# Loading the last columns of a batched matmul trace through another DMA queue

What was changed: the last 640 columns of the last B tile are loaded in float32 by SyncE instead of in bf16 by GpSimd, not before the last whole rows have landed, and VectorE multiplies them as they are.

## Chip, cores, metric

The program uses one core of one Trainium2 chip; its runs were spread over several chips, so each time is compared with the kernel before in the same rounds on the same chip. The metric is the device time of a run in microseconds (us). "Span" is the time from the first to the last instruction of the one profiled execution; it lies about 1.8 us below the run's time. PE is TensorE, PSUM the memory that it writes to, and a load has "landed" when the profile shows it complete. Times to a hundredth of a us that no printed line shows were read from the packed traces.

## The reference

```python
B, N = 8, 2176
prod = np.matmul(a, b)                                    # a, b: (8, 2176, 2176) float32
traces = np.diagonal(prod, axis1=1, axis2=2).sum(axis=-1) # (8,)
```

Only the trace is wanted, so each result is the sum of A-transposed times B, element by element: 2 x 151.5 MB are read once, and a handful of operations fall on each element.

## The kernel before

A is loaded with a cast to bf16 by GpSimd, transposed on PE into PSUM and copied ("evacuated") to `at`. B is loaded the same way. In the last batch B's products are shared: VectorE multiplies and sums (`multiply_reduce`, one column of `late` or `acc` per product), and PE accumulates 128x128 products in `trace_ps`, whose diagonal VectorE takes by a product with the identity. The last B row tile arrives in three pieces:

```python
LAST_PIECES = [(0, 2), (2, 3), (3, 5)]            # in units of 512 columns: 1024, 512, 640
...
for g0, g1 in LAST_PIECES:
    lo, hi = g0 * WIDE, min(g1 * WIDE, N)
    nc.gpsimd.dma_start(out=row[:, lo:hi], in_=b[bi, start:start + P, lo:hi])
multiply_on_pe(at, row, v0, 0, 1)
late.append((wide_at(at, v0, 1, 2), wide(row, 1, 2)))            # 512 columns on VectorE
for g in range(2, n_wide):                                        # 256 of each later 512
    half = ROWS // 2
    multiply_on_pe(at, row, v0, g, g + 1, rows=half)
    late.append((wide_at(at, v0, g, g + 1)[:, half:, :], wide(row, g, g + 1)[:, half:, :]))
multiply_on_pe(at, row, v0, n_wide, len(a_groups))
...                                                               # (cut)
for n, (x, y) in enumerate(late):
    multiply_reduce(x, y, late_acc[:, n:n + 1])
multiply_reduce(tiles[f32], trace_ps, late_acc[:, len(late):len(late) + 1])
...                                                               # sum over partitions on PE
nc.vector.tensor_copy(out=tiles["result"][:1, :BATCH], in_=total) # the "result copy"
nc.sync.dma_start(out=..., in_=tiles["result"][:1, :BATCH])       # the output
```

## Time and profile before

| | before |
|---|---|
| time, median of 4 runs | 711.43 us (711.36 to 711.58) |
| span of the profiled run | 709.8 us |
| HBM read over the span | 427 GB/s |
| VectorE / PE busy | 58% / 33% |
| last GpSimd piece seen / result copy / output issued | 705.60 / 706.91 / 707.10 us |

Read it like this: DMA bounds the whole stream, and the only part in which this change can alter the time is the last 7 us. The lines stand in the prediction.

### The profile page before, as it was taken

How to read it: one execution, taken by the hardware profiler on the slowest of the kernel's cores; microseconds unless marked ns; L12 is line 12 of the kernel's file. 1: busy time of each engine (PE TensorE's matmuls, PEld its weight loads, DVE VectorE, ACT ScalarE, POOL GpSimd, SP SyncE). 2: the span in 40 equal slices, each digit the busy share in tenths (PEclk: the TensorE clock that was granted, in tenths of full speed). 3: DMA queues.
4: the chain of work that ended last, by engine and by line, in shares of the span. 5: the costliest groups of instructions: out<-in, count | busy, mean ns of one | idle time of the engine just before them, and what ended most of it. 6: DMA issues, size and time to landing. Idle time of an engine off the chain costs nothing.

```text
span 709.8 us, 3800 instructions
## 1 busy us (share of the span) xinstructions
PE 233.3 (33%) x1406; PEld 221.8 (31%) x1406; DVE 408.9 (58%) x449; ACT 201.6 (28%) x210; POOL 45.2 (6%) x91
## 2 busy tenths in 40 slices
PE   2660025600345003540036400374003630036356
PEld 1660025600344003540036400374003630036355
DVE  0327972279812898219972199621996319963146
ACT  2651015600256002550035500354003630036300
POOL 2000000000000000000000000000000000000010
PEclk9866556755588555885556755666556875567755
DMA  9999999999999999999999999999999999999997
GB/s 220 220 220 219 206 219 219 220 218 206 221 219 218 218 210 218 220 218 214 213 219 219 218 213 214 220 218 216 213 217 219 218 216 212 218 218 216 219 210 139
DMA packets 12116, 152.32 MB, mean 215 GB/s; under 512 B 1346, under 2 KB 1602, under 8 KB 3778
## 3 DMA queue, kind: packets, MB, share of 16 engines
q0 software_dynamic: 11952, 150.97, 100.1%
q1 hardware_dynamic: 146, 1.11, 0.4%
q8 instruction: 11, 0.18, 0.1%
q14 instruction: 7, 0.06, 0.0%
HBM read 303.04 MB, written 0.00 MB: 427 GB/s over the span
## 4 chain that ended last, share of the span: by engine, by line
DMA 52%; issue 43%; POOL 3%; PE 2%; DVE 1%; another core or an unknown queue 0%; POOLq 0%; DVEq 0%
DMA t<-in_a_dram 42%; DMA t<-in_b_dram 6%; DMA b_t<-in_b_dram 3%; POOL t L57 2%; PE ps L136 1%; PE trace_ps L256 1%; DVE scratch L103 0%; DVE at L91 0%; POOL b_t L222 0%; POOLq L57 0%; PE ps L157 0%; POOL identity masks.py:199 0%; PE total L271 0%; POOL identity masks.py:197 0%
## 5 line engine op out<-in xcount | busy, mean ns | idle before, releaser
L103 DVE CUSTOM_DVE_ANT_1 scratch<-at,t 128x2048 bf16<-128x2048 bf16 (+1 forms) x156 | 310.5, 1990 | 85.5 <-DMA t<-in_b_dram 78.9
L136 PE MATMUL ps<-identity,t 128*128 128x128 f32 x1071 | 204.2, 372 | 460.3 <-DMA t<-in_a_dram 297.7
L136 PEld LDWEIGHTS ps<-identity,t 128*128 128x128 f32 x1071 | 193.7, 218 | 468.3 <-issue 302.8
L93 ACT COPY at<-ps 128x1024 bf16<-128x1024 bf16 x208 | 199.2, 1016 | 471.2 <-PE ps L136 471.1
L91 DVE COPY at<-ps 128x1024 bf16<-128x1024 bf16 (+2 forms) x104 | 92.8, 902 | 205.8 <-PE ps L136 198.9
L57 POOL DMA_DIRECT2D t<-in_a_dram x39 | 20.8, 535 | 329.5 <-DVE acc L103 230.2
L57 POOL DMA_DIRECT2D t<-in_b_dram x41 | 21.7, 530 | 304.2 <-PE ps L157 286.5
L256 PEld LDWEIGHTS <-at 128*128 128x128 bf16 x153 | 17.4, 124 | 12.0 <-issue 12.0
L256 PE MATMUL trace_ps<-t,at 128*128 128x128 bf16 x144 | 17.3, 294 | 10.2 <-DMA t<-in_b_dram 10.2
L157 PE MATMUL ps<-identity,t 128*128 128x128 bf16 x170 | 17.0, 224 | 2.2 <-DVE at L91 2.2
L157 PEld LDWEIGHTS <-t 128*128 128x128 bf16 x170 | 13.4, 102 | 3.8 <-issue 3.4
L103 DVE DVE_READ_ACCUMULATOR2_ANT acc<- 128x1 f32 x163 | 13.3, 82 | 0.0
L68 DVE CAST t<-words 128x1088 bf16<-128x1088 f32 x1 | 0.7, 726 | 4.9 <-DMA words<-in_a_dram 4.9
L103 DVE CUSTOM_DVE_ANT_0 scratch<-at,t 128x128 bf16<-128x128 bf16 x7 | 2.0, 291 | 0.2
L67 ACT CAST t<-words 128x1088 bf16<-128x1088 f32 x1 | 1.1, 1098 | 3.7 <-DMA words<-in_a_dram 3.7
L222 POOL DMA_DIRECT2D b_t<-in_b_dram x3 | 1.6, 539 | 3.6 <-PE trace_ps L256 3.6
L256 PE MATMUL trace_ps<-b_t,at 128*128 128x128 bf16 x9 | 1.5, 287 | 0.5 <-DMA b_t<-in_b_dram 0.4
L103 DVE CUSTOM_DVE_ANT_1 scratch<-at,b_t 128x256 bf16<-128x256 bf16 (+1 forms) x3 | 1.5, 510 | 0.2 <-DMA b_t<-in_b_dram 0.2
L248 DVE TENSOR_REDUCE sums<-acc 128x1 f32<-128x22 f32 (+1 forms) x8 | 1.4, 174 | 0.3
L67 ACT ACT_TABLE_LOAD x1 | 1.3, 1283 | 0.7 <-PEq L294 0.7
L271 PE MATMUL total<-late,ones 128*1 128x1 f32 x8 | 0.5, 163 | 0.3 <-DVE late L103 0.3
masks.py:199 POOL TENSOR_SCALAR_AFFINE_SELECT identity<-identity 128x128 f32<-128x128 f32 (+1 forms) x2 | 0.6, 308 | 0.0
(14 smaller groups left out, 2.4 us busy)
## 6 DMA issues: line engine op xcount, KB each, us to landing
t<-in_a_dram POOLq DMA_DIRECT2D x32, 2176.0 KB, 42.3
t<-in_b_dram POOLq DMA_DIRECT2D x31, 2176.0 KB, 47.2
t<-in_b_dram POOLq DMA_DIRECT2D x9, 544.0 KB, 39.5
t<-in_a_dram POOLq DMA_DIRECT2D x7, 544.0 KB, 35.0
words<-in_a_dram SPq DMA_DIRECT2D x1, 1088.0 KB, 5.0
t<-in_b_dram POOLq DMA_DIRECT2D x1, 1088.0 KB, 41.7
b_t<-in_b_dram POOLq DMA_DIRECT2D x1, 256.0 KB, 23.0
b_t<-in_b_dram POOLq DMA_DIRECT2D x1, 160.0 KB, 23.4
```

The lines of the kernel that those rows point to most:

```text
L57: issued = nc.gpsimd.dma_start(out=t[:, 0:m, :], in_=rows)
L67: nc.scalar.copy(out=t[:, 0, :half], in_=plain[:, :half])
L68: nc.vector.tensor_copy(out=t[:, 0, half:], in_=plain[:, half:])
L91: nc.vector.tensor_copy(out=dst, in_=src)
L93: nc.scalar.copy(out=dst, in_=src)
L103: nc.vector.tensor_tensor_reduce(out=out, in0=x, in1=y, scale=1.0, scalar=0.0, op0=MUL, op1=ADD, accum_out=acc,)
L136: nc.tensor.transpose(ps[:, n * m + r, :], words[:, r, c0:c0 + step * (P - 1) + 1:step], tiles[f32],)
L157: last_transpose = nc.tensor.transpose(ps16[:, n, r, :], a_t[:, r, c0:c0 + P], tiles[bf16],)
L222: nc.gpsimd.dma_start(out=row[:, lo:hi], in_=b[bi, start:start + P, lo:hi])
L248: nc.vector.reduce_sum(out=tiles["sums"][:, bi:bi + 1], in_=acc[:, :cols], axis=mybir.AxisListType.X)
L256: nc.tensor.matmul(trace_ps, x, y, start=(n == 0), stop=(n == len(pe_work) - 1),)
L271: nc.tensor.matmul(total[:, BATCH - 1:BATCH], tiles["ones"], part, start=(n == 0), stop=(n == len(parts) - 1),)
```

## The change

The intent: the last piece no longer needs PE and the accumulated matrix after it, and no longer goes through GpSimd's queue. Cut to its core:

```diff
-    LAST_PIECES = [(0, 2), (2, 3), (3, 5)]
+    LAST_ROUNDED = [(0, 1024), (1024, 1536)]
+    LAST_PLAIN = [(1536, 1920), (1920, N)]
+    plain_pool = ctx.enter_context(tc.tile_pool(name="plain", bufs=1))
...  # transpose_group: the last row of at is evacuated in column order (step of four elements)
+            if v0 == natural and m > 1:
+                in_order = at[:, v0, start:start + P * m].rearrange("q (p r) -> q r p", r=m)
+                evacuate(in_order, ps16[:, 0, :, :])
...  # last tile
+                for lo, hi in LAST_ROUNDED:
                     nc.gpsimd.dma_start(out=row[:, lo:hi], in_=b[bi, start:start + P, lo:hi])
+                    half = (lo + hi) // 2
+                    for c in range(lo, half, P):
+                        pe_work.append((at[:, v0, c:c + P], row[:, c:c + P]))
+                    late.append((at[:, v0, half:hi], row[:, half:hi]))
+                plain = plain_pool.tile([P, N - base], f32, tag="plain")
+                for lo, hi in LAST_PLAIN:
+                    begun = nc.sync.dma_start(out=plain[:, lo - base:hi - base], in_=b[bi, ..., lo:hi])
+                    tc.add_manual_dep(begun.ins, last_rows.ins.name, ...)   # after the last whole rows
+                    final.append((at[:, v0, lo:hi], plain[:, lo - base:hi - base]))
...  # after the identity product
+    for n, (x, y) in enumerate(final, len(late) + 1):
+        multiply_reduce(x, y, late_acc[:, n:n + 1])
```

More of the change, by code (lines that the diff above doesn't have):

```diff
@@ L80, in constants @@
         sums = const.tile([P, BATCH], f32, tag="sums")
-        late = const.tile([P, 4], f32, tag="late")
+        late = const.tile([P, 8], f32, tag="late")
         result = const.tile([P, BATCH], f32, tag="result")
@@ L111, with transpose_group @@
     split = n_wide * WIDE
-    def transpose_group(at, a_t, start, m, b_groups):
+    def transpose_group(at, a_t, start, m, b_groups, natural=None):
         words = a_t[:, :, :].bitcast(f32)
@@ L150, in transpose_group @@
                 evacuate(dst[:, v0:v0 + 2, :, :], halves[:, 0, :, :, :])
-        for at0 in range(0, len(singles), 8 // m):
-            some = singles[at0:at0 + 8 // m]
+        chunks = [singles[n:n + 8 // m] for n in range(0, len(singles), 8 // m)]
+        for some in chunks:
             ps = psum_pool.tile([P, 4, P], f32, tag="aT")
@@ L162, in transpose_group @@
             v0 = some[0][0]
-            evacuate(dst[:, v0:v0 + len(some), :, :], ps16[:, 0:len(some), :, :])
+            if v0 == natural and m > 1:
+                assert len(some) == 1
+                in_order = at[:, v0, start:start + P * m].rearrange("q (p r) -> q r p", r=m)
+                evacuate(in_order, ps16[:, 0, :, :])
+            else:
+                evacuate(dst[:, v0:v0 + len(some), :, :], ps16[:, 0:len(some), :, :])
         return last_transpose
@@ L184, in multiply_on_pe @@
                 ))
-    late = []
+    late, final = [], []
     ahead = None
@@ L204 @@
                 a_t, _ = load(a[bi], start, m)
-            last_transpose = transpose_group(at, a_t, start, m, b_groups)
+            last_transpose = transpose_group(
+                at, a_t, start, m, b_groups, natural=NT - 1 if last else None
+            )
         acc = acc_pool.tile([P, 2 * NT], f32, tag="acc")
@@ L219 @@
                 row = b_t[:, 0, :]
-                for g0, g1 in LAST_PIECES:
-                    lo, hi = g0 * WIDE, min(g1 * WIDE, N)
+                for lo, hi in LAST_ROUNDED:
                     nc.gpsimd.dma_start(out=row[:, lo:hi], in_=b[bi, start:start + P, lo:hi])
-                multiply_on_pe(at, row, v0, 0, 1)
-                late.append((wide_at(at, v0, 1, 2), wide(row, 1, 2)))
-                for g in range(2, n_wide):
-                    half = ROWS // 2
-                    multiply_on_pe(at, row, v0, g, g + 1, rows=half)
-                    late.append((
-                        wide_at(at, v0, g, g + 1)[:, half:, :], wide(row, g, g + 1)[:, half:, :]
-                    ))
-                multiply_on_pe(at, row, v0, n_wide, len(a_groups))
+                    half = (lo + hi) // 2
+                    for c in range(lo, half, P):
+                        pe_work.append((at[:, v0, c:c + P], row[:, c:c + P]))
+                    late.append((at[:, v0, half:hi], row[:, half:hi]))
+                base = LAST_PLAIN[0][0]
+                plain = plain_pool.tile([P, N - base], f32, tag="plain")
+                for lo, hi in LAST_PLAIN:
+                    begun = nc.sync.dma_start(
+                        out=plain[:, lo - base:hi - base], in_=b[bi, start:start + P, lo:hi]
+                    )
+                    tc.add_manual_dep(
+                        begun.ins, last_rows.ins.name,
+                        mybir.DependencyInfo(
+                            mybir.DependencyClass.Sync, mybir.DependencyReason.DATA
+                        ),
+                        reason="after the last whole rows",
+                    )
+                    final.append((at[:, v0, lo:hi], plain[:, lo - base:hi - base]))
                 continue
-            b_t, _ = load(b[bi], start, m)
+            b_t, last_rows = load(b[bi], start, m)
             for s in range(m):
@@ L268 @@
     )
-    parts = [tiles["sums"][:, BATCH - 1:BATCH]] + [late_acc[:, n:n + 1] for n in range(len(late) + 1)]
+    parts = [tiles["sums"][:, BATCH - 1:BATCH]] + [late_acc[:, n:n + 1] for n in range(len(late) + 1 + len(final))]
     for n, part in enumerate(parts):
```

## The prediction

> **What bounds the kernel now.** I read the page first: one core streams both inputs once, the DMA engines are full until the last slice, and no compute engine is over 58% busy.
>
> ```profile
> span 709.8 us, 3800 instructions
> PE 233.3 (33%) x1406; PEld 221.8 (31%) x1406; DVE 408.9 (58%) x449; ACT 201.6 (28%) x210; POOL 45.2 (6%) x91
> DMA  9999999999999999999999999999999999999997
> HBM read 303.04 MB, written 0.00 MB: 427 GB/s over the span
> ```
>
> 303 MB at 427 GB/s is the whole span. The change moves no byte of the first 98.9%, so only what follows the last bulk transfer can change. That part I read in the chain that ended last, in order of time:
>
> ```profile
> 682.21 23.39 DMA b_t<-in_b_dram
> 705.60 0.04 issue
> 705.64 0.50 PE trace_ps L256 x3
> ...
> 706.34 0.29 DVE scratch L103
> ```
>
> The three pieces of the last B row tile are issued at 681.2 to 682.2 and sit 23 us in a full queue. The last one counts as landed at 705.60; then come three matmuls, VectorE's product of the accumulated 128x128 matrix with the identity, and the sum. VectorE's own timeline shows how much room there is:
>
> ```profile
> 703.04 1.23 DVE L103 CUSTOM_DVE_ANT_1 scratch<-at,t 128x1024 bf16<-128x1024 bf16 x1 [1.40 <-DMA t<-in_b_dram]
> 704.39 0.68 DVE L103 CUSTOM_DVE_ANT_1 scratch<-at,b_t 128x512 bf16<-128x512 bf16 x1
> 705.11 0.42 DVE L103 CUSTOM_DVE_ANT_1 scratch<-at,b_t 128x256 bf16<-128x256 bf16 x1
> 705.46 0.08 DVE L103 DVE_READ_ACCUMULATOR2_ANT late<- 128x1 f32 x1
> 705.72 0.42 DVE L103 CUSTOM_DVE_ANT_1 scratch<-at,b_t 128x256 bf16<-128x256 bf16 x1 [0.18 <-DMA b_t<-in_b_dram]
> 706.34 0.29 DVE L103 CUSTOM_DVE_ANT_0 scratch<-identity,trace_ps 128x128 bf16<-128x128 f32 x1 [0.18 <-PE total L271]
> 706.91 0.15 DVE L275 COPY result<-total 1x8 f32<-1x8 f32 x1 [0.28 <-PE total L271]
> ```
>
> From the moment the last whole row has landed (703.04) VectorE is almost never idle: 0.18 us before the last piece, 0.18 us before the identity product, then the unavoidable wait for the final sum. The chain names a DMA and PE, but VectorE runs 0.36 us behind nothing. Any column added to it in this stretch costs time as soon as those 0.36 us are used up.
>
> The DMA queue in the same stretch (slices of 0.1 us from 702 to 706):
>
> ```profile
> DMA  7998899999896876656633233322222100000000
> ```
>
> The engines do not finish together. Individual packets in the trace (their byte sizes name the piece) say the same: packets of the last piece run from 702.02 on the earliest engine to 705.28 on the latest. Last packets end at 702.58 for the last whole row, 703.83 for columns 0 to 1023, 704.48 for 1024 to 1535, 705.28 for 1536 to 2175. Compute reacts 0.3 to 0.5 us after that (705.28 to 705.60; 702.58 to 703.04).
>
> **What the Trainium skill says.** "DMA: Bandwidth & Descriptors", section "Issuing engines are not separate DMA queues": DMAs started from any engine run on the same 16 DMA engines, and starting them elsewhere saves only issue time. So SyncE brings no bandwidth; the kernel before cannot show it, as SyncE moves only 1.1 MB at the start. Same page, "The descriptor swizzle": a transfer to 128 partitions is split over the engines the same way by SyncE's path as by GpSimd's, so I expect the late engines to keep their share of the moved columns. Same page, "Latency and other measured facts": first byte about 0.6 us after the issue for SyncE. The trace differs a little: the first-tile load is issued at 0.74 and its first packet starts at 1.77 (1.03 us); the output at 707.10, first packet 707.84 (0.74 us). I use 0.75 to 1.05. "VectorE: DVE Perf Modes", section "The perf-mode tier table": a two-tensor op runs twice as fast in bf16 as in float32. That would make a float32 operand dear, but the fused multiply-and-sum here is not at the fast rate in bf16: mean durations by shape are 2.291 us for 2048 elements, 1.226 for 1024, 0.692 for 512, 0.424 for 256, which is 1.04 ns per element plus about 0.16. It takes one element per cycle already, and the identity product, whose inputs are float32, takes 0.29 for 128, on the same line. So I charge float32 nothing extra.
>
> **The change part by part.**
>
> *Removed.* The third GpSimd piece, 640 columns. Its packets took 116 ns, eight per engine, spaced some 0.1 us: about 0.8 us on each engine, which is the 704.48 to 705.28 above. Also removed: three of PE's nine matmuls of this row (six remain, all before column 1536), and VectorE's second 256-column product.
>
> *Added on DMA.* Two float32 loads of 384 and 256 columns, 0.33 MB, the same bytes read from HBM as before. They wait for the last whole row, so SyncE issues the first at about 702.95. With 0.32 to 0.40 us per issue (both SyncE issues of the trace), the second goes at 703.3. First packets at 703.7 to 704.0 and 704.05 to 704.35. By then the early engines have been empty for about a microsecond, and the late ones are still in columns 1024 to 1535. The late engines decide: they have the same bytes left, so they end at about 705.3 as before, perhaps 0.1 to 0.3 later; the data counts as landed at 705.6 to 705.9. Where the two queues share a late engine, columns 1024 to 1535 are held up by some packets, I estimate 0.2 to 0.4 us: last packet near 704.8, seen at 705.2.
>
> *Added on VectorE.* Products of 384 and 256 columns instead of one of 256. The net addition is 384: 384 x 1.04 + 0.16 = 0.56 us, 0.58 from start to next start (0.72 was observed for 512, 0.43 for 256).
>
> *The new end.* 512 columns start at 704.39 as now. The 256 of the second piece could start at 705.11; I put 705.2 for the sharing above. Then 0.43: the identity product starts at 705.63 without waiting, since PE ends its two matmuls of that piece near 705.5. Then 0.29: the 384 columns at 705.92. Then 0.58: the 256 columns at 706.50, done with the accumulator read at 706.93. The result copy comes 0.28 us after that read's end (706.63 to 706.91 before): 707.21, against 706.91. That is 0.30 us later. The data it needs is there: 705.92 and 706.50 against landings of about 705.4 and 705.6 to 705.9. Check by sums: added 0.58, minus the two waits of 0.18 it fills, is 0.22, plus 0.09 for the late second piece: 0.31.
>
> *Beside the path.* The last row of the transposed A is now written in column order by four evacuations of 512 elements with a step of four elements. They took 0.42 us each; at one element per cycle it would be 512 x 1.04 + 0.16 = 0.69, so 4 x 0.27 = 1.1 us in all, at 640 to 675 us, where the queue holds 23 us or more of issued transfers. Nothing of it reaches the end. One more column sum on PE lies in the shadow of VectorE.
>
> **The rivals.**
>
> *VectorE stays hidden and the end follows the landing.* The intent of the change must be this: after the last byte, no matmul, no accumulated matrix, only one short product. Before, landing to result copy takes 706.91 - 705.60 = 1.31 us; after, it could be 0.42 + 0.08 + 0.28 = 0.8. If the early-finished GpSimd queue also made VectorE's start at 703.04 earlier, the change would gain up to 0.5 us: 711.0. Against it: VectorE's chain from 703.04 leaves only 0.36 us, and the last whole row's landing is not touched.
>
> *The held-back load becomes the wait.* If SyncE's latency under load is that of the start with its slow transfer (5.0 us from issue to landing for 1.1 MB, of which 3.6 us lie between first and last packet, so 1.4 us is fixed), 702.95 + 0.4 + 1.4 + 0.8 for the bytes = 705.55: still before 706.50. It needs a further microsecond to matter. If the packets on the late engines take turns badly, the end could slip by 0.5 to 1 us: 712.3 to 712.7.
>
> *The float32 operand is slower on VectorE.* Were it half speed, 640 x 1.04 = 0.67 us more: 712.4. Against it: the 1.04 ns per element at both types.
>
> **Range and chances.** 711.46 + 0.30 = 711.76. The three runs of before spread by 0.18 us, and the edges come from the rivals, with room for a difference between chips and runs: 711.0 to 712.6. Two per cent is 14.2 us, twice everything that follows the last landing, so faster or slower by that much would need the bulk stream to change: chances 0.003 and 0.005.
>
> **What would show it.** Right: VectorE without a wait between the 512-column product and the final sum; last products of 384 and 256 at 0.56 and 0.42 us starting near 705.9 and 706.5; SyncE's first issue at 702.9 to 703.0; result copy near 707.2. Wrong: a wait of VectorE for the float32 tile (the second rival), a 256-column product well over 0.42 us (the third), a result copy before 706.9 (the first), or the last whole row landing at another time than 702.6 to 703.0, which would mean that the stream itself was disturbed.

## The result and the profile after

711.32 us, median of 4 runs (711.20 to 711.35), against 711.43. The ratio is 0.9998, 95% interval 0.9981 to 1.0015: the same. (Ratios are the mean time of one kernel's runs over that of the other's of the same rounds, so not quite the ratio of the medians quoted.) The prediction was 711.76 with a range of 711.0 to 712.6. The measured time lies in that range, but on the other side of the kernel before: 0.30 us more was forecast, and the medians show 0.11 us less.

VectorE's and SyncE's timeline of the changed kernel from the last whole row on (start us, duration us, instruction, and in brackets the idle time before it and what ended it; VectorE's short accumulator reads, its small reduction at 704.24 and the rows of PE are left out):

```profile
702.86 0.80 SPq L241 DMA_DIRECT2D plain<-in_b_dram  x2
702.97 1.23 DVE L105 CUSTOM_DVE_ANT_1 scratch<-at,t 128x1024 bf16<-128x1024 bf16 x1 [1.38 <-DMA t<-in_b_dram]
704.31 0.68 DVE L105 CUSTOM_DVE_ANT_0 scratch<-at,b_t 128x512 bf16<-128x512 bf16 x1
705.04 0.42 DVE L105 CUSTOM_DVE_ANT_0 scratch<-at,b_t 128x256 bf16<-128x256 bf16 x1
705.64 0.29 DVE L105 CUSTOM_DVE_ANT_0 scratch<-identity,trace_ps 128x128 bf16<-128x128 f32 x1 [0.17 <-DVE late L105]
705.98 0.56 DVE L105 CUSTOM_DVE_ANT_0 scratch<-at,plain 128x384 bf16<-128x384 bf16 x1
706.58 0.43 DVE L105 CUSTOM_DVE_ANT_0 scratch<-at,plain 128x256 bf16<-128x256 bf16 x1
707.29 0.15 DVE L298 COPY result<-total 1x8 f32<-1x8 f32 x1 [0.28 <-PE total L294]
707.48 0.32 SPq L299 DMA_DIRECT2D out_dram<-result  x1
```

This is the chain of the prediction to within 0.1 us: issue at 702.86 (702.95 was forecast), no wait for the float32 tile, products of 384 and 256 at 705.98 and 706.58 (705.92 and 706.50), result copy at 707.29 (707.21). How errors cancel in it is told below. The result is ready 0.38 us *later* than before. Yet the span is 0.35 us *shorter* (709.43 against 709.78). These are single executions: the profiled run of the kernel before took 711.54 us, 0.11 above its median, and that of the changed kernel 711.20, its fastest, so 0.35 us overstates the gain in the medians. But a later result without a longer span is not what the prediction allows. So the end of the program is not the output.

What stands after the output is neither in the chain of waits nor in the busy times, since semaphore and drain instructions are not counted as busy. It shows when one asks for the instructions of the line that closes the program (L305 before, L328 after, the `with tile.TileContext` around the kernel). Columns: engine, operation, count, duration in ns as minimum/median/maximum, first and last start in us. Before:

```profile
L305 POOLq EVENT_SEMAPHORE  x4: 17/17/17, 709.1 to 709.7; - x4
L305 POOLq DRAIN  x3: 45/95/27027, 682.0 to 709.5; - x3
L305 SPq DRAIN  x3: 7/7/7, 708.2 to 709.3; - x3
```

After:

```profile
L328 POOLq EVENT_SEMAPHORE  x4: 17/17/17, 708.7 to 709.3; - x4
L328 POOLq DRAIN  x3: 45/96/26687, 681.5 to 709.2; - x3
L328 SPq DRAIN  x3: 7/7/7, 708.6 to 708.9; - x3
```

GpSimd's last load is issued at 682.2 us (681.6 in the changed kernel), and by then its sequencer has begun a `DRAIN` instruction. Before, that drain starts at 682.00 and lasts 27.027 us, to 709.03. SyncE, which waits for the output to be written, has arrived at 708.31 and waits 0.72 us for GpSimd. GpSimd's first semaphore instruction starts at 709.07, and the program is over 0.71 us after that. I take it for the one that collects the engines, since it starts 0.02 to 0.05 us after the later of the two arrivals in every trace. In the changed kernel the drain ends at 681.49 + 26.69 = 708.18, before SyncE arrives at 708.69, and the collecting starts at 708.71. The drain ended 0.85 us earlier; the last packet of GpSimd's queue came at 704.46 instead of 705.28, 0.82 us earlier. That is the size of the 640 columns taken out of that queue.

My theory, then (called theory A in the expectations): **the program ends about 0.74 us after the later of two arrivals. One is GpSimd's drain, which ends 3.7 us after the last packet of GpSimd's DMA queue; the other is SyncE, 1.39 us after the result copy.** Before, the drain was later by 0.72 us, so VectorE had that much slack. The rivals: the span follows the result copy (B); the drain depends on the number of loads that GpSimd issued, not on when the queue empties (C); or the gain comes from PE's part and not from who loads.

The DMA queue over the last us (702 to 706, slices of 0.1 us) after:

```profile
DMA  9787684784673331325988799999973200000000
```

It falls to 1 to 3 tenths from 703.2 to 703.8, fills again when SyncE's packets arrive (the first at 703.81, 0.95 us after the issue), and is empty at the same time as before: last packet of the last columns 705.29, against 705.28. And as landing times of the two loads, KB and us from issue to landing:

```profile
plain<-in_b_dram SPq DMA_DIRECT2D x1, 192.0 KB, 2.4
plain<-in_b_dram SPq DMA_DIRECT2D x1, 128.0 KB, 2.3
```

So the data did not come earlier by the other queue. Only GpSimd's own queue ended earlier.

### The profile page after: what moved, and what is told of

Same layout as the page of the kernel before. It is cut to its first block, busy times and chain, and to the rows that moved or that the text cites. A ratio compares the mean times of both kernels' runs of the same rounds, so it can differ in the third digit from the quotient of the medians.

```text
span 709.4 us, 3803 instructions
## 1 busy us (share of the span) xinstructions
PE 229.9 (32%) x1405; PEld 218.1 (31%) x1405; DVE 412.6 (58%) x451; ACT 201.2 (28%) x210; POOL 44.5 (6%) x90
## 4 chain that ended last, share of the span: by engine, by line
DMA 52%; issue 43%; POOL 2%; DVE 1%; PE 1%; another core or an unknown queue 0%; POOLq 0%; DVEq 0%
DMA t<-in_a_dram 42%; DMA t<-in_b_dram 10%; POOL t L59 2%; PE ps L141 1%; DVE scratch L105 1%; DVE at L93 0%; POOLq L59 0%; POOL identity masks.py:199 0%; POOL identity masks.py:197 0%; DVE late L105 0%; PE ps L162 0%; PE total L294 0%; DVE sums L269 0%; DVE result L298 0%
## 5 line engine op out<-in xcount | busy, mean ns | idle before, releaser
L141 PE MATMUL ps<-identity,t 128*128 128x128 f32 x1071 | 201.0, 368 | 463.2 <-DMA t<-in_a_dram 299.4
L141 PEld LDWEIGHTS ps<-identity,t 128*128 128x128 f32 x1071 | 190.3, 218 | 471.6 <-issue 304.6
L93 DVE COPY at<-ps 128x1024 bf16<-128x1024 bf16 (+2 forms) x104 | 95.9, 935 | 202.9 <-PE ps L141 196.7
```

What stands on the lines that cost most here:

```text
L93: nc.vector.tensor_copy(out=dst, in_=src)
L141: nc.tensor.transpose(ps[:, n * m + r, :], words[:, r, c0:c0 + step * (P - 1) + 1:step], tiles[f32],)
```

## The experiments

All of them gave correct results, and all are timed in five rounds beside the kernel before. The effects are some tenths of a us in 711, and no interval of the ratios (about plus or minus 0.0013) is narrow enough to separate them; what tells the theories apart are the arrival times in the traces, which are sharp to some hundredths, and the medians agree with them. The kernel before was traced once, but its nine runs on each of the three chips have spans of 709.6 to 710.2, with a median of 709.8 every time, so its trace is a fair measure on all of them. One caution: the bulk stream itself arrives earlier or later by up to 0.3 us from one execution to the next (VectorE sees the last whole row between 702.90 and 703.22 in traces in which nothing before it differs), and that moves everything behind it.

### One more product on VectorE, kernel before (e1_before_delay)

```diff
-        late = const.tile([P, 4], f32, tag="late")
+        late = const.tile([P, 8], f32, tag="late")
+    multiply_reduce(late[0][0], late[0][1], late_acc[:, 7:8])     # never used
     multiply_reduce(tiles[f32], trace_ps, late_acc[:, len(late):len(late) + 1])
```

> The kernel before, with one more VectorE product (512 columns, its result never used) ahead of the identity product. VectorE then runs 0.72 us longer, of which it had 0.18 free: the result copy should come at about 707.45 instead of 706.91. Theory A (the program ends when GpSimd's own drain at the end is through, about 3.74 us after the last packet of its DMA queue, and the output leaves 0.74 us of slack beside it): GpSimd's drain ends at 709.0 as before, span 709.8, no change of the time (ratio 1.0000, within 0.0002). Theory B (the span follows the result copy at a fixed distance, and the drain only happens to lie there): span 710.3, ratio about 1.0008.

Measured: 711.55 us, before 711.55, ratio 1.0000 (0.9987 to 1.0012). The result copy came 0.62 us later, and the span is 709.65 us, not longer than before:

```profile
706.95 0.29 DVE L103 CUSTOM_DVE_ANT_0 scratch<-identity,trace_ps 128x128 bf16<-128x128 f32 x1 [0.18 <-DVE late L103]
...
707.53 0.15 DVE L276 COPY result<-total 1x8 f32<-1x8 f32 x1 [0.28 <-PE total L272]
```

```profile
L306 POOLq DRAIN  x3: 45/87/27162, 681.8 to 709.4; - x3
```

SyncE arrives at 708.91 and the drain ends at 708.91: the slack is exactly used up. Theory B falls. The first line shows something else: here PE had finished the accumulated matrix at 706.02, and still VectorE stood 0.18 us before the identity product. So that gap, which I had counted as a wait for PE that could be filled, is not one.

### The same product, changed kernel (e2_after_delay)

```diff
+    multiply_reduce(late[0][0], late[0][1], late_acc[:, 7:8])     # never used
     multiply_reduce(tiles[f32], trace_ps, late_acc[:, len(late):len(late) + 1])
```

> The changed kernel with the same unused 512-column product ahead of the identity product. VectorE has no free time there, so the result copy should move from 707.29 to about 708.0. Theory A: here the output sets the end (GpSimd's drain ends at 708.18, the output's side at 708.69), so all 0.72 us show: span 710.15, ratio to before about 1.0005. Theory B: the same 0.72 us more than the changed kernel. A third reading, that the changed kernel still ends with its DMA and VectorE has room: span 709.4.

Measured: 712.01 us, ratio to before 1.0005 (0.9992 to 1.0019), result copy at 708.15, span 710.28. Of the 0.86 us by which the copy is later than in the changed kernel's trace, 0.13 are the stream's (its last packet of GpSimd's queue is at 704.59 instead of 704.46), the rest is the product. The span grew by 0.85. In the changed kernel VectorE is on the path in full; in the kernel before it was not.

### Fewer loads, the same bytes in GpSimd's queue (e3_two_pieces)

```diff
-    LAST_PIECES = [(0, 2), (2, 3), (3, 5)]
+    LAST_PIECES = [(0, 2), (2, 5)]
```

> The kernel before with the last tile in two GpSimd loads (1024 and 1152 columns) instead of three. The last packet of GpSimd's queue should stay at about 705.28, the late columns be seen only at 705.6, the result copy come at about 707.1 to 707.2. Theory A (drain ends a fixed 3.7 us after the last packet of the queue): drain ends at 709.0, span 709.8, ratio 1.000. Theory C (the drain is shorter in the changed kernel because GpSimd has issued one load fewer): drain ends near 708.2 and the span falls to about 709.2 to 709.4, ratio 0.9993 or so.

Measured: 711.45 us, ratio 0.9999 (0.9986 to 1.0011), span 709.8. GpSimd issued two loads for the last tile, as in the changed kernel, and its drain ended at 681.49 + 27.60 = 709.08:

```profile
L305 POOLq DRAIN  x3: 45/87/27596, 681.5 to 709.6; - x3
```

The last packet was at 705.38, so the distance is 3.71 us. Theory C falls. (The result copy came at 707.48, later than I expected, since the late columns were all seen only at 705.8; it costs nothing here.)

### The changed kernel with GpSimd's loads (e4_gpsimd_load)

```diff
-                    begun = nc.sync.dma_start(out=plain[:, ...], in_=b[bi, start:start + P, lo:hi])
-                    tc.add_manual_dep(begun.ins, last_rows.ins.name, ...)
-                    final.append((at[:, v0, lo:hi], plain[:, lo - base:hi - base]))
+                    nc.gpsimd.dma_start(out=row[:, lo:hi], in_=b[bi, start:start + P, lo:hi])
+                    final.append((at[:, v0, lo:hi], row[:, lo:hi]))
```

> The changed kernel without its SyncE part: columns 1536 to 2175 are again loaded in bf16 by GpSimd, in two loads of 384 and 256, and all of them multiplied by VectorE in the order of the changed kernel. VectorE's chain should be that of the changed kernel, result copy at 707.3. Theory A: the last packet of GpSimd's queue is back at about 705.3, its drain ends at 709.0, span 709.8, no gain over before. Rival (the gain, if any, comes from taking the last matmuls off PE, not from who loads): span 709.4 as in the changed kernel.

Measured: 711.73 us against 711.55, ratio 1.0002 (0.9989 to 1.0015). Drain and SyncE:

```profile
L317 POOLq DRAIN  x3: 45/87/26647, 682.6 to 709.7; - x3
L317 SPq DRAIN  x3: 7/7/7, 708.8 to 709.5; - x3
```

SyncE arrived at 708.86, the drain ended at 709.24, 3.75 us after the last packet at 705.49; span 710.0. The stream was 0.2 us later in this trace, which is the 0.2 above my 709.8. Rearranging the products alone gains nothing; taking the columns out of GpSimd's queue is what gains. The run also settles the float32 question: VectorE's 384 columns take 558 ns with bf16 data here, 559 ns with float32 data in the changed kernel.

### More of the tile by SyncE (e5_less_gpsimd)

```diff
-    LAST_ROUNDED = [(0, 1024), (1024, 1536)]
-    LAST_PLAIN = [(1536, 1920), (1920, N)]
+    LAST_ROUNDED = [(0, 1024)]
+    LAST_PLAIN = [(1024, 1536), (1536, N)]
```

> The changed kernel with columns 1024 to 2175 (512 and 640) loaded by SyncE, so that GpSimd's queue ends with columns 0 to 1023. Theory A: last packet of GpSimd's queue at about 703.8, its drain ends at 707.5 and binds nothing; the output sets the end. VectorE: 512 columns to 705.03, identity product to 705.32, wait for the first float32 tile to about 705.4, 512 and 640 columns, result copy at about 707.3, span 709.4 to 709.55, as in the changed kernel. If the drain were not tied to the last packet (a fixed time of the program), it would still end at 708.2 or later.

Measured: 711.76 us against 711.57, ratio 1.0004 (0.9990 to 1.0018), span 709.8. The drain moved as expected: last packet 703.95, drain over at 707.63, 3.68 us, though the last whole row was seen no earlier than in the changed kernel. But the result was later than I wrote (707.70 where 707.3 was expected). About 0.25 us of that had gathered before the first float32 product, from a stream 0.13 us later than in the changed kernel's trace and the 0.18 us gap before the identity product; the rest is that the second load is now a wait:

```profile
706.59 0.82 DVE L105 CUSTOM_DVE_ANT_0 scratch<-at,plain 128x640 bf16<-128x640 bf16 x1 [0.24 <-DMA plain<-in_b_dram]
```

```profile
L328 POOLq DRAIN  x3: 45/96/26433, 681.2 to 709.6; - x3
```

The second load took 3.1 us from issue to landing for 320 KB, where I had taken it as already there. Result copy 707.70, SyncE 709.09. Of what SyncE loads after the last whole row, 640 columns arrived in time here and 1152 did not.

### Not holding the loads back (e6_no_hold)

```diff
-                    tc.add_manual_dep(begun.ins, last_rows.ins.name, ...)
```

> The changed kernel without holding the SyncE loads back: they are issued in the first microseconds. Their 0.33 MB then go before the bulk stream, which should move everything after it by 0.33 MB at 427 GB/s, 0.77 us: last whole row seen at about 703.7 instead of 702.97, last packet of GpSimd's queue at 705.2, its drain at 708.95, VectorE's chain without a wait and the result copy at about 708.0. Theory A: the output sets the end, span about 710.1, 0.7 us more than the changed kernel. If holding back is worth nothing (the stream has slack somewhere, or the data being there early helps VectorE), span 709.4 or less.

Measured: 712.16 us against 711.57, ratio 1.0009 (0.9997 to 1.0022), span 710.3. SyncE issued its loads at 1.18 us; the last whole row was seen at 703.85 instead of 702.97, the result copy came at 708.18. That fits the expectation that the bytes go ahead of the stream and push it back: 0.88 us against 0.77 expected, with the 0.3 us of caution. Without the hold the change would lose: all five runs (712.07 at least) are above all nine of the kernel before (711.71 at most), though the interval of the ratio includes 1.

### Attempts at a better version (e7_reordered, e8_one_load, and once more)

e7 gives columns 1024 to 1535 to PE alone and puts the first float32 product ahead of the identity product; e8 has the first of these, and a single float32 load of 640 columns.

```diff
-                    half = (lo + hi) // 2                              # e7, e8
+                    half = (lo + hi) // 2 if lo == 0 else hi
...                                                                         # (cut: no empty product)
-    LAST_PLAIN = [(1536, 1920), (1920, N)]                             # e8 only
+    LAST_PLAIN = [(1536, N)]
+    products = late + final[:1] + [(tiles[f32], trace_ps)] + final[1:] # e7 only
```

> An attempt at a better version: all of columns 1024 to 1535 go to PE, and VectorE takes the first float32 tile ahead of the identity product. VectorE: 512 columns to 705.03, wait for the first float32 tile to about 705.35, 384 columns to 705.93, identity product to 706.22, 256 columns, result copy at about 706.93. Theory A: output's side done at 708.33, GpSimd's drain at 708.2, span 709.05, 0.35 us under the changed kernel and 0.7 under before (ratio 0.9990). Theory B (span follows the result copy at before's distance): 709.8.

> As the reordered version, with a single float32 load and product of 640 columns (an instruction less on VectorE), after the identity product or ahead of it as the order gives: late product of 512, float32 product of 640, identity product. The float32 tile should be seen at about 705.6, 640 columns take 0.83 us to 706.45, identity product to 706.75, result copy at about 707.0, span 709.1: within 0.1 us of the reordered version.

Measured: e7 711.07 us (711.00 to 711.09), ratio 0.9993 (0.9981 to 1.0006), span 709.2. e8 710.91 us (710.86 to 710.96), ratio 0.9991 (0.9978 to 1.0003), span 709.2; before 711.57 (711.40 to 711.71). In e8 the identity product stands ahead of the float32 one (the expectation has it the other way round, a slip of mine):

```profile
705.59 0.29 DVE L105 CUSTOM_DVE_ANT_0 scratch<-identity,trace_ps 128x128 bf16<-128x128 f32 x1 [0.51 <-PE total L295]
705.92 0.82 DVE L105 CUSTOM_DVE_ANT_0 scratch<-at,plain 128x640 bf16<-128x640 bf16 x1
707.03 0.15 DVE L299 COPY result<-total 1x8 f32<-1x8 f32 x1 [0.28 <-PE total L295]
```

SyncE arrives at 708.42, the drain ends at 708.21. In e7 it is 708.50 and 708.12; the 0.17 us gap before the identity product, which I had again not counted, is most of the 0.18 us by which its result copy misses the expectation.

The changed kernel, e8 and a variant of e8 then ran on one chip. The variant gives 128 columns back to VectorE, which idles 0.51 us before the identity product:

```diff
-                    half = (lo + hi) // 2 if lo == 0 else hi
+                    half = (lo + hi) // 2 if lo == 0 else hi - P
```

> The changed kernel itself once more, five rounds beside the kernel before, to have its time on the same chip as the best version. From the end of its own trace (drain at 708.2, output's side done at 708.7, plus 0.71) against before (drain at 709.03) theory A puts it 0.35 us under before: ratio 0.9995; its first four runs gave 0.11 us (0.9998).

> The version with a single float32 load, with 128 of columns 1024 to 1535 given back to VectorE, which stood idle for 0.51 us before the identity product, so that PE is done one matmul (0.13 us) earlier. VectorE: 512 to 705.07, 128 to 705.36, identity product at about 705.45, 640 columns at 705.77, result copy 706.88. Output's side done at 708.27, GpSimd's drain at 708.21: both ends meet. Theory A: span 709.0 to 709.05, 0.1 to 0.15 us under the one-load version, 0.7 to 0.75 under before (ratio 0.9990); nothing is left to gain from VectorE then.

> The one-load version again, for comparison on the same chip: span 709.15, ratio to before 0.9991, about 0.25 us under the changed kernel.

Measured, before at 711.61 us (711.48 to 711.84): the changed kernel 711.34 (711.12 to 711.36), ratio 0.9995 (0.9983 to 1.0008); the variant 711.08 (710.93 to 711.25), 0.9992; e8 711.05 (710.79 to 711.12), 0.9991 (0.9977 to 1.0005). The variant is a miss, 0.03 us above e8 in the medians where 0.1 to 0.15 below was expected: the identity product still started 2.54 us after VectorE saw the last whole row, against 2.55 in e8 on the same chip, as the 128-column product filled the idle time and the usual 0.17 us gap came behind it. e8 has the lowest medians; e7 and the variant are not told apart from it with certainty. Its ten runs (711.12 at most) all lie below the 18 runs of before beside them (711.40 at least), although the intervals of the ratios still include 1.

### All arrivals together

Times in us from the traces, rounded, so that a difference can be off by 0.01. "Last packet" is the end of the last data packet of GpSimd's queue.

| kernel | last packet | drain over | distance | result copy | SyncE arrives | span |
|---|---|---|---|---|---|---|
| before | 705.28 | **709.03** | 3.74 | 706.91 | 708.31 | 709.78 |
| changed | 704.46 | 708.18 | 3.72 | 707.29 | **708.69** | 709.43 |
| e1 | 705.19 | **708.91** | 3.73 | 707.53 | **708.91** | 709.65 |
| e2 | 704.59 | 708.30 | 3.72 | 708.15 | **709.54** | 710.28 |
| e3 | 705.38 | **709.08** | 3.71 | 707.48 | 708.87 | 709.82 |
| e4 | 705.49 | **709.24** | 3.75 | 707.47 | 708.86 | 709.99 |
| e5 | 703.95 | 707.63 | 3.68 | 707.70 | **709.09** | 709.83 |
| e6 | 705.31 | 708.99 | 3.68 | 708.18 | **709.56** | 710.29 |
| e7 | 704.40 | 708.12 | 3.73 | 707.11 | **708.50** | 709.23 |
| e8 | 704.48 | 708.21 | 3.73 | 707.03 | **708.42** | 709.15 |
| e9 (changed again) | 704.41 | 708.12 | 3.71 | 707.24 | **708.62** | 709.35 |
| e10 | 704.72 | 708.43 | 3.71 | 707.22 | **708.61** | 709.34 |
| e11 (e8 again) | 704.58 | 708.31 | 3.73 | 707.14 | **708.54** | 709.28 |

The later arrival is bold. In every row the span is that arrival plus 0.72 to 0.75; the drain follows the last packet by 3.68 to 3.75; SyncE follows the result copy by 1.38 to 1.40. Last packets 1.55 us apart and one to four GpSimd loads for the last tile fit the same distance.

## Why the prediction was right or wrong

- **The bulk stream is untouched, so the change is within 2%:** right. 427 GB/s before and after. (The comparison beside it is loose: 14.2 us is twice the 6.7 us from the last whole row to the end, and more than three times the 4.2 us after the last landing.)
- **SyncE's loads:** right. First issue expected at about 702.95 and found at 702.86; first packet 0.95 us after the start of the issue (0.75 to 1.05 expected), 0.63 us after its end at 703.18; end of the last packet 705.29 (about 705.3, perhaps later); no wait of VectorE for them.
- **Sharing holds columns 1024 to 1535 up by 0.2 to 0.4 us:** wrong. Their last packet was at 704.46 against 704.48 before, and the term of 0.09 us in the sum was nothing. The packets were not slowed either: from 703.8 us on, when SyncE's begin, 25 of them were still to start (26 before), and they took 98 ns each in both kernels. Why the two queues did not get in each other's way I have not tested.
- **Float32 costs VectorE nothing extra:** right, 559 against 558 ns for 384 columns.
- **VectorE's sum:** near by luck. The copy came 0.38 us later than before where 0.30 was forecast, but with errors that offset each other. Set against the prediction's own steps, the second piece's 256 columns started 0.16 us earlier (705.04 for 705.2: nothing held them up, and the last whole row happened to be seen 0.07 us earlier). Then 0.17 us were lost, because one of the two waits of 0.18 could not be filled: the gap before the identity product is 0.17 to 0.18 us in e1 and in the changed kernel too, with PE done (what it is stays open). The identity product took 0.34 us from its start to the next one's, where the prediction charged its bare duration of 0.29, and the 384 columns 0.60 where it charged 0.58. Together that is 0.08 us more than forecast.
- **"Landing to result copy", and from the result copy to the end a constant: this step failed.** "711.46 + 0.30 = 711.76" carried the later copy straight through to the time. The distance from result copy to the end of the span was 2.87 us before and 2.13 after. The end before was set by GpSimd's drain, with 0.72 us of slack for the output. What followed: +0.38 us fitted into that slack, and the drain, the real end, came earlier until SyncE's arrival took over: 709.03 to 708.69, 0.34 us. Of these 0.34 us, 0.07 are the earlier stream of that one execution. The prediction's first rival has a gain of up to 0.5 us, but from an earlier VectorE; its mechanism did not occur. (Its 0.8 us from landing to result copy counts the accumulator read twice: the read overlaps the product, and 706.58 to 707.29 is 0.71.) So it is luck that the measured time lies inside the range: the range reached down to 711.0 for the sake of that rival, and no path that the prediction named leads to the end that was found.
- **The evacuation in column order:** off the path, as said, but mis-sized. The four copies took 1288 ns each, not 690: together 3.5 us more than before instead of the estimated 1.1 (1288 ns for 512 elements is over twice the multiply's 1.04 ns per element on which the estimate rests). VectorE's copies around 635 to 685 us, before and after (mean ns behind the comma):

```profile
L91 DVE COPY at<-ps 128x512 bf16<-128x512 bf16 x4 | 1.7, 421 | 0.5 <-PE ps L157 0.5
```

```profile
L93 DVE COPY at<-ps 128x512 bf16<-128x512 bf16 x4 | 5.2, 1288 | 0.5 <-PE ps L162 0.5
```

How much of the 0.35 us in the spans is a gain in time to rely on? The medians show 0.11 us in the first comparison and 0.27 in the second, both inside intervals of more than 0.8 us either way. In both, every run of the changed kernel (711.35 and 711.36 at most) lies below every run of the kernel before beside it (711.36 and 711.48 at least), which speaks for a gain of that order. That the mechanism acts is shown by the arrivals; the size of the gain is not better known than that.

## What to carry to other kernels

In a short tail, look at what the program does after its last useful instruction: the chain of waits that the profile prints stops at the output, while the instructions that close the program may still wait for an engine's DMA queue. Here the queue of GpSimd should run empty about 2.3 us before the result is ready (3.72 of drain less the output's 1.39), so the last bytes belong to another queue, held back until the bulk is through and few enough to land in time. And before a gap ahead of an instruction is counted as room, check that it vanishes when the instruction it waits for is done.

## What the Trainium skill lacked or had wrong

- No page gives the time of GpSimd's drain at the end of a program. "Runtime: NRT & Kernel Launch", section "The launch sequence", lists barriers, a semaphore reset and a reset of the DMA rings behind the kernel, but not that GpSimd's drain is over only 3.68 to 3.75 us after the last packet of its DMA queue, nor that SyncE arrives 1.38 to 1.40 us after the result copy. The drains around the kernel that "VectorE: DVE Perf Modes", section "The DRAIN you can't avoid", mentions as short and constant on all five engines are not like this one of 26.4 to 27.6 us.
- "VectorE: DVE Perf Modes", the section "The perf-mode tier table", has two-tensor operations in bf16 at twice the float32 rate. The fused multiply-and-sum used here has no row there: 1.04 ns per element, and 558 ns (bf16) against 559 ns (one operand float32) for 384 elements.
- The same page gives no cost for a copy out of PSUM that writes with a step of four bf16 elements: 1288 ns for 512 elements, against 421 ns when it writes them in runs of 128. The costs of scattered writes that I found, in "Vector Engine (DVE) Microarchitecture Reference", are for 4-byte words.
- "DMA: Bandwidth & Descriptors", section "Latency and other measured facts": about 0.6 us to the first byte for SyncE's loads, without saying from where it counts. Here the first packet came 0.95 us after the start of the issue, but 0.63 us after its end, which agrees with the page; to landing it was 2.3 to 2.4 us for 128 and 192 KB.
